# Two halves of a softmax exchange set four units of work apart, eight more buffer units, and gate tiles in another order

## The chip, the cores and the metric

The kernel runs on one core of a Trainium2 chip. A core has TensorE (PE, the matmuls; PEld is its weight load), VectorE (DVE), ScalarE (ACT), GpSimd (POOL) and SyncE (SP). Each engine works through a queue of its own in a fixed order, waits on semaphores at the head of that queue, and ACT and SP also issue DMAs from theirs. The metric is the device time of one execution in microseconds (us). The table below has the median of three timed runs and one more execution that was profiled.

## The reference

Two transformer blocks run one after the other on one sequence of 512 rows of 1024 numbers, all in float32. The first has two layers (forget-gate attention, then retention, each beside a cross-attention to 256 memory rows). The second block, where the change lies, computes:

```python
q, k, v, glu_in, gates = split(rms_norm(x, g) @ w_in)
outs, m, l = three attention groups, dilations 1, 4, 16 (4 heads each)
w = l * exp(m - max over groups of m)       # per row and head
a = sum over groups of (w * o) / sum over groups of w
y_a = a @ w_attn_out
c = silu(layer_norm(causal_conv31(val * sigmoid(gate of glu_in))))
y_c = c @ conv_pw_w
g_a, g_c = split(sigmoid(gates + b_gate))
x = x + rms_norm((g_a * y_a + g_c * y_c) @ w_out)
...                                          # then a gated feed-forward
```

The maxima `m` and the sums `l` of the three groups meet in one weight for each row and head. Group 0 (the "band") holds its rows in sequence order, 128 rows to a partition block; groups 1 and 2 (dilated) hold them by residue of the row number. So the statistics have to change layout between the groups, and the kernel does that through DRAM.

## The kernel before, in words

All large products are done as three matmuls on high and low parts of the operands (`mm3`, L208 to L215; `add_nat`, L422 to L424). Every weight cut comes in by a DMA on SP's queue into `ring_w` (L314), ACT casts its high part into `ring_hl` (L324), DVE subtracts to get the low part (L326), and then one PE unit of 24 matmuls uses it. `ring_hl` has two slots of two cuts, so casts run at most a few units ahead of PE. An evacuation into high and low parts (`evac_hl`, L204) is one ACT cast (L205) and one DVE subtraction (L206).

Side work is recorded in chains. `push([...])` makes a chain of steps, and `run_bg` takes one step from the chains after each unit; `nop` is a step that does nothing and lets a unit pass. `drain` takes all that is left. What a step records is then placed on each engine's queue by a scheduler with a model of its own of when each instruction will be ready, so the queues don't stand exactly as the steps were recorded.

For each of four heads `j` (0 to 3), the q, k and v tiles are computed, then `push_softmax(j)` starts a chain: scores of the dilated groups (their input copied by L1442, matmul L1501, maxima L1504, exponentials L1487), band scores (maxima L1524, L1487), and then the steps this case is about:

- `swap_out`, L1540 and L1541: four DMAs on ACT's queue. L1540 writes the band's maxima and sums to DRAM (`xn<-small`, 2 KB in 512 elements of 4 bytes), L1541 those of the dilated groups (`xp<-small`); each once for the maxima (k = 0) and once for the sums (k = 1).
- `swap_in`, L1549 and L1550: four DMAs on ACT's queue that read them back in the other layout (`small<-xn`, `small<-xp`). They wait at the head of ACT's queue until the write has landed.
- `weigh`: the weights, by DVE (L1556 to L1565) with one exponential on ACT for each of two halves (L1560), then the scaling of the probabilities (POOL L1574, L1577, ACT L1580).
- `tr` and `mul`: transposes (L1596; `tr_band`, L1647 to L1650, evacuated by L205 and L206) and the products with v (L1616; `pv_band`, with `mm3`). Their order on the list puts groups 1 and 2 first, the band last.

Beside these, DVE runs the pieces of the 31-tap convolution (L1418), sigmoids of ACT (L1382 for the gated linear unit, L1771 for the gates) evacuate PE's units, and `FS` is a pool of buffer units for 128x512 float32 (`arena_f`, N_F of them).

Of the kernel before, what the change touches and what calls it, by code (L numbers as in the profile page):

```python
# [33 lines left out]
TW = 384  # L34

N_R = 50
N_F = 23
N_HL = 2


# [60 lines left out]
def tile_kernel(ctx: ExitStack, tc: tile.TileContext, a: dict, out: bass.AP, stop_at=None):  # L101
    nc = tc.nc
# [6 lines left out]
    arena_r = cpool.tile([P, N_R, 512], F32R, name="arena_r")  # L109
    arena_f = cpool.tile([P, N_F, 512], F32, name="arena_f")  # L110
    ring_w = cpool.tile([P, 2, 2048], F32, name="ring_w")
# [3 lines left out]
    RS = Slots([arena_r[:, i] for i in range(N_R)], "R")  # L115
    FS = Slots([arena_f[:, i] for i in range(N_F)], "F")
    WS = Slots([ring_w[:, i] for i in range(2)], "W")
# [3 lines left out]
    def hl():  # L121
        return HL(RS.get(), RS.get())
# [50 lines left out]
    def vc(i):  # L173
        return vec[:, i : i + 1]
# [29 lines left out]
    def evac_hl(src, h, l):  # L204
        nc.scalar.copy(h, src)  # L205
        nc.vector.tensor_sub(l, src, h.bitcast(F32))  # L206

    def mm3(ps, pairs, start=True, stop=True, check=True):  # L208

        n = len(pairs)  # L210
        for k, (wh, wl, xh, xl) in enumerate(pairs):
            o = {} if check else {"skip_group_check": True}
            nc.tensor.matmul(ps, wh, xh, start=start and k == 0, stop=False, **o)  # L213
            nc.tensor.matmul(ps, wh, xl, start=False, stop=False, **o)  # L214
            nc.tensor.matmul(ps, wl, xh, start=False, stop=stop and k == n - 1, **o)  # L215
# [79 lines left out]
    def push(steps):  # L295
        c = Chain(steps)
        chains.append(c)
        return c
# [89 lines left out]
    def wsrc(w, r0, nr, c0, ncol):  # L388
        return w[r0 : r0 + nr, c0 : c0 + ncol].rearrange("(k p) c -> p k c", p=P)

    def add_proj(w, c0, x, evacs, n=512):


        def unit(i):
            def f(h, l):
                ps = PA.get()
                sl = slice(i * P, (i + 1) * P)
                mm3(ps[:, 0:n], [(h[:, k, sl], l[:, k, sl], x()[k].h[:, 0:n], x()[k].l[:, 0:n]) for k in range(KC)])
                evacs[i](ps)
                ps.free()  # L400

            return f

        ncol = P * len(evacs)
        all_jobs.append(
            Job([((A, A, slice(0, ncol)), wsrc(w, 0, D, c0, ncol))], (8, 256), CUT2[: len(evacs)],
                [unit(i) for i in range(len(evacs))])
        )
# [46 lines left out]
    def add_call(f):  # L455
        all_jobs.append(Job(None, None, None, [f]))
# [203 lines left out]
    getx = lambda: G["h"]  # L660
# [576 lines left out]
    w2 = a["w_in_2"][0]  # L1237
# [231 lines left out]
    def by_residue(ap):  # L1469

        return ap.rearrange("p (t r) -> p r t", r=4)

    def stats(j, g):

        key = ("st", j, min(g, 1))
        if key not in G:
            G[key] = SM.get()
        return G[key]
# [55 lines left out]
    def push_softmax(j):  # L1534
        def swap_out():

            n, r = stats(j, 0), stats(j, 1)
            for k in range(2):
                c = 12 * k
                nc.scalar.dma_start(xn[j, k].rearrange("(i p) -> p i", p=P), n[:, c : c + 4])  # L1540
                nc.scalar.dma_start(  # L1541
                    xp[j, k].rearrange("g (p r) -> p g r", r=4), r[:, c + 4 : c + 12].rearrange("p (g r) -> p g r", g=2)
                )

        def swap_in():
            n, r = stats(j, 0), stats(j, 1)
            for k in range(2):
                c = 12 * k
                nc.scalar.dma_start(r[:, c : c + 4], xn[j, k].rearrange("(p r) -> p r", r=4))  # L1549
                nc.scalar.dma_start(n[:, c + 4 : c + 12], xp[j, k].rearrange("g (i p) -> p (g i)", p=P))  # L1550

        def coef(g):

            st = stats(j, g)
            top, tot = st[:, 24:28], st[:, 28:32]
            nc.vector.tensor_max(top, st[:, 0:4], st[:, 4:8])  # L1556
            nc.vector.tensor_max(top, top, st[:, 8:12])
            m3 = st[:, 0:12].rearrange("p (g i) -> p g i", g=3)
            nc.vector.tensor_sub(m3, m3, top.unsqueeze(1).to_broadcast([P, 3, 4]))
            nc.scalar.activation(st[:, 0:12], st[:, 0:12], AF.Exp, scale=SCALE)  # L1560
            nc.vector.tensor_mul(st[:, 12:24], st[:, 12:24], st[:, 0:12])
            nc.vector.tensor_add(tot, st[:, 12:16], st[:, 16:20])
            nc.vector.tensor_add(tot, tot, st[:, 20:24])
            nc.vector.reciprocal(tot, tot)
            nc.vector.tensor_mul(m3, m3, tot.unsqueeze(1).to_broadcast([P, 3, 4]))  # L1565

        def norm(g):

            st = stats(j, g)
            us = G[("p", g, j)][0]  # L1570
            if g:
                u, c = us[0].ap, st[:, 4 * g : 4 * g + 4]
                u3 = u.rearrange("p (r q) -> p r q", r=4)
                nc.gpsimd.tensor_mul(u3, u3, c.unsqueeze(2).to_broadcast([P, 4, P]))  # L1574
            else:
                u3 = us[0].ap.rearrange("p (i q) -> p i q", i=2)
                nc.gpsimd.tensor_mul(u3, u3, st[:, 2:4].unsqueeze(2).to_broadcast([P, 2, 256]))  # L1577
                for i in (1, 0):
                    p = G[("p", g, j)][1][i]
                    nc.scalar.activation(p, p, AF.Copy, scale=st[:, i : i + 1])  # L1580

        def weigh():
            coef(1)
            norm(1)
            norm(2)
            coef(0)
            norm(0)
            for i in range(2):
                G.pop(("st", j, i)).free()

        def tr(g):
            u, p = G.pop(("p", g, j))
            if g:
                ps = PA.get()
                for r in range(4):
                    nc.tensor.transpose(ps[:, r * P : (r + 1) * P], p[r], ident)  # L1596
                t = FS.get()
                nc.scalar.copy(t.ap, ps.ap)
                ps.free()
                G[("pt", g, j)] = t  # L1600
            else:
                G[("pt", g, j)] = tr_band(p)
            for x in u:
                x.free()

        def mul(g):
            v = G[("v", g, j // 2)]
            pt = G.pop(("pt", g, j))
            if g == 1:
                G[("av", j)] = PA.get()  # L1610
            ps = G[("av", j)]
            if g:
                o = by_residue(ps.ap)
                for r in range(4):
                    c = (r % 2) * 256 + (j % 2) * P
                    nc.tensor.matmul(  # L1616
                        o[:, r], v[r // 2][:, c : c + P], pt[:, r * P : (r + 1) * P],
                        start=g == 1 and r == 0, stop=False, skip_group_check=True,
                    )
                pt.free()  # L1620
            else:
                pv_band(v, j % 2, pt, ps)
            if j % 2:
                for x in G.pop(("v", g, j // 2)):
                    x.free()
            if g == 0:
                ps = G.pop(("av", j))
                t = hl()
                evac_hl(ps.ap, t.h, t.l)
                ps.free()  # L1630
                G[("a", j)] = t

        push([
            swap_out, nop, swap_in, nop, weigh, nop,
            lambda: (tr(1), tr(2)), lambda: (mul(1), mul(2)), lambda: tr(0), lambda: mul(0),
        ])

# [117 lines left out]
    def add_block2():  # L1755
# [12 lines left out]
        def eg(c, f):  # L1768
            def ev(ps):
                t = FS.get()  # L1770
                nc.scalar.activation(t.ap, ps.ap, AF.Sigmoid, bias=vc(V_BG + c * 8 + f))  # L1771
                G[("sg", c, f)] = t

            return ev
# [37 lines left out]

        for t in range(4):
            add_proj(w2, 6656 + t * 256, getx, [eg(0, 2 * t), eg(0, 2 * t + 1)])
            if t == 3:
                add_call(flush)
        half_a(0)
        half_a(1)

# [20 lines left out]
            return ev  # L1840

        getc = lambda: G["c"]
        gate = lambda t: add_proj(w2, 7680 + t * 256, getx, [eg(1, 2 * t), eg(1, 2 * t + 1)])
        gate(0)
        gate(1)
        add_call(drain)
        for t in range(4):
            add_proj(a["conv_pw_w_2"][0], t * 256, getc, [ev_c(2 * t), ev_c(2 * t + 1)])
            if t < 2:
                gate(t + 2)  # L1850
            if t == 1:
                add_call(free_h)

        def free_c():
# [433 lines left out]
```

## Time and profile before

| | us |
|---|---|
| timed runs | 1913.97, 1913.65, 1907.75 (median 1913.65) |
| profiled execution | 1909.46, its span 1907.8 |
| PE busy | 1855.4 (97% of the span) |
| DVE, ACT, POOL busy | 1142.7, 825.7, 354.7 |

PE is busy nearly all the time. What is not work of PE is some 52 us in small pieces, and in the middle of the second block the four head chains are the place where PE waits. A row of a timeline gives the start, the length, the engine, the line and the operation, and in brackets how long the engine had been idle and what ended that.

### The profile page before, as it was taken

How to read it: one execution, taken by the hardware profiler on the slowest of the kernel's cores; microseconds unless marked ns; L12 is line 12 of the kernel's file. 1: busy time of each engine (PE TensorE's matmuls, PEld its weight loads, DVE VectorE, ACT ScalarE, POOL GpSimd, SP SyncE). 2: the span in 40 equal slices, each digit the busy share in tenths (PEclk: the TensorE clock that was granted, in tenths of full speed). 3: DMA queues.
4: the chain of work that ended last, by engine and by line, in shares of the span. 5: the costliest groups of instructions: out<-in, count | busy, mean ns of one | idle time of the engine just before them, and what ended most of it. 6: DMA issues, size and time to landing. Idle time of an engine off the chain costs nothing. (4 is left out here: it accounts for less than half of the span.)

```text
span 1907.8 us, 24620 instructions
## 1 busy us (share of the span) xinstructions
PE 1855.4 (97%) x9759; PEld 1588.2 (83%) x9759; DVE 1142.7 (60%) x1752; ACT 825.7 (43%) x1395; POOL 354.7 (19%) x324
## 2 busy tenths in 40 slices
PE   7899999999989999999999999989999999999998
PEld 7688888888888888898878988968888887888886
DVE  7644544344474566756569797969365386554555
ACT  5444433444354645445253324324363455333342
POOL 1110100110031133433361101010031242100101
PEclk9999999999999999999999999989999999999999
DMA  6342232232223232323223534542553213323221
GB/s 207 106 128 89 78 100 89 78 99 90 89 94 122 72 100 81 97 79 98 77 82 115 171 96 77 116 101 89 172 171 111 89 67 103 108 89 111 88 89 66
DMA packets 200373, 194.57 MB, mean 102 GB/s; under 512 B 22199, under 2 KB 171574, under 8 KB 200258
## 3 DMA queue, kind: packets, MB, share of 16 engines
q1 hardware_dynamic: 184386, 192.90, 32.4%
q10 hardware_dynamic: 15872, 0.10, 0.7%
q8 instruction: 76, 1.25, 0.3%
q14 instruction: 39, 0.32, 0.1%
HBM read 182.40 MB, written 12.94 MB: 102 GB/s over the span
## 5 line engine op out<-in xcount | busy, mean ns | idle before, releaser
L213 PE MATMUL psum<-arena_r,ring_hl 128*128 128x512 f32 (+1 forms) x1936 | 746.8, 387 | 9.5 <-ACT ring_hl L324 8.6
L215 PE MATMUL psum<-arena_r,ring_hl 128*128 128x512 f32 (+1 forms) x1936 | 741.3, 383 | 6.3 <-DVE ring_hl L326 6.3
L214 PE MATMUL psum<-arena_r,ring_hl 128*128 128x512 f32 (+1 forms) x1936 | 740.8, 383 | 3.4 <-DVE arena_r L627 2.6
L326 DVE TENSOR_TENSOR ring_hl<-ring_w,ring_hl 128x1024 fp32r<-128x1024 f32 (+2 forms) x306 | 393.9, 1294 | 284.5 <-ACT ring_hl L324 279.2
L324 ACT CAST ring_hl<-ring_w 128x1024 fp32r<-128x1024 f32 (+2 forms) x307 | 316.4, 1037 | 511.7 <-PE psum L214 330.8
L213 PEld LDWEIGHTS psum<-arena_r,ring_hl 128*128 128x128 f32 x1936 | 367.0, 190 | 79.4 <-ACT ring_hl L324 9.0
L215 PEld LDWEIGHTS psum<-arena_r,ring_hl 128*128 128x128 f32 x1936 | 366.7, 189 | 79.1 <-DVE ring_hl L326 8.5
L214 PEld LDWEIGHTS psum<-arena_r,ring_hl 128*128 128x128 f32 x1936 | 367.1, 190 | 73.1 <-DVE arena_r L627 3.3
L422 PE MATMUL psum<-ring_hl,arena_r 128*128 128x256 f32 x640 | 183.8, 287 | 2.2 <-ACT ring_hl L324 2.2
L424 PE MATMUL psum<-ring_hl,arena_r 128*128 128x256 f32 x640 | 182.9, 286 | 0.3 <-DVE ring_hl L326 0.3
L1418 DVE SCALAR_TENSOR_TENSOR arena_f<-cpad,vec,arena_f 128x512 f32<-128x512 f32 x240 | 180.5, 769 | 3.7
L423 PE MATMUL psum<-ring_hl,arena_r 128*128 128x256 f32 x640 | 182.7, 285 | 0.0
L422 PEld LDWEIGHTS psum<-ring_hl,arena_r 128*128 128x128 f32 x640 | 124.6, 195 | 3.4 <-ACT ring_hl L324 2.6
L423 PEld LDWEIGHTS psum<-ring_hl,arena_r 128*128 128x128 f32 x640 | 124.5, 195 | 0.5
L424 PEld LDWEIGHTS psum<-ring_hl,arena_r 128*128 128x128 f32 x640 | 124.3, 194 | 0.6 <-DVE ring_hl L326 0.6
L206 DVE TENSOR_TENSOR arena_r<-psum,arena_r 128x512 fp32r<-128x512 f32 (+2 forms) x136 | 78.7, 607 | 69.0 <-ACT arena_r L205 68.9
L205 ACT CAST arena_r<-psum 128x512 fp32r<-128x512 f32 (+2 forms) x136 | 66.5, 526 | 95.6 <-PE psum L215 38.3
L205 ACT CAST arena_r<-arena_f 128x512 fp32r<-128x512 f32 (+1 forms) x78 | 46.2, 598 | 116.9 <-POOL arena_f L1962 67.3
L926 POOL TENSOR_SCALAR arena_f<-arena_f,small 128x512 f32<-128x512 f32 (+3 forms) x48 | 33.9, 725 | 307.8 <-DVE small L924 302.5
L206 DVE TENSOR_TENSOR arena_r<-arena_f,arena_r 128x512 fp32r<-128x512 f32 (+1 forms) x78 | 53.3, 689 | 60.2 <-ACT arena_r L205 59.5
L606 POOL TENSOR_TENSOR arena_f<-arena_f 128x512 f32<-128x512 f32 x40 | 63.7, 1604 | 99.3 <-ACT arena_f L601 97.0
L1962 POOL TENSOR_TENSOR arena_f<-arena_f 128x512 f32<-128x512 f32 x22 | 32.0, 1455 | 262.2 <-DVE arena_f L1938 247.8
(240 smaller groups left out, 2078.0 us busy)
## 6 DMA issues: line engine op xcount, KB each, us to landing
ring_w<-in_fox_w_in SPq DMA_DIRECT2D x28, 1024.0 KB
ring_w<-in_w_in SPq DMA_DIRECT2D x22, 1024.0 KB
ring_w<-in_w_up SPq DMA_DIRECT2D x22, 1024.0 KB
ring_w<-in_w_out SPq DMA_DIRECT2D x20, 1024.0 KB
ring_w<-in_ret_w_in SPq DMA_DIRECT2D x16, 1024.0 KB
ring_w<-in_w_in SPq DMA_DIRECT2D x24, 512.0 KB
ring_w<-in_w_down SPq DMA_DIRECT2D x10, 1024.0 KB
ring_w<-in_w_mem_kv SPq DMA_DIRECT2D x8, 1024.0 KB
```

The source lines that it names most:

```text
L205: nc.scalar.copy(h, src)
L206: nc.vector.tensor_sub(l, src, h.bitcast(F32))
L213: nc.tensor.matmul(ps, wh, xh, start=start and k == 0, stop=False, **o)
L214: nc.tensor.matmul(ps, wh, xl, start=False, stop=False, **o)
L215: nc.tensor.matmul(ps, wl, xh, start=False, stop=stop and k == n - 1, **o)
L324: nc.scalar.copy(j.hv[sl], v[sl])
L326: (nc.gpsimd if j.done in j.spare else nc.vector).tensor_sub(lo, v[sl], j.hv[sl].bitcast(F32))
L422: nc.tensor.matmul(o, c.h[:, sl], h[:, k, :], start=k == 0, stop=False)
L423: nc.tensor.matmul(o, c.l[:, sl], h[:, k, :], start=False, stop=False)
L424: nc.tensor.matmul(o, c.h[:, sl], l[:, k, :], start=False, stop=k == n - 1)
L606: nc.gpsimd.tensor_add(acc, acc, t.ap)
L1418: nc.vector.scalar_tensor_tensor(t, src, wk, t, ALU.mult, ALU.add)
```

## The change

N_F goes from 23 to 31, with the memory for eight more units from a smaller scratch area of dynamic DMAs. The chain of a head gets two more empty steps between writing the statistics out and reading them in, and two more between reading them in and weighing. In the gate tiles the first goes before `flush`, and the other three are spread as the diff shows. No instruction of PE, DVE, POOL or SP is added or removed; ACT gets four more table loads, and instructions stand in another order.

```diff
--- before.py
+++ after.py
@@ -34,7 +34,7 @@
 TW = 384
 
 N_R = 50
-N_F = 23
+N_F = 31
 N_HL = 2
 
 
@@ -1631,7 +1631,7 @@
                 G[("a", j)] = t
 
         push([
-            swap_out, nop, swap_in, nop, weigh, nop,
+            swap_out, nop, nop, nop, swap_in, nop, nop, nop, weigh, nop,
             lambda: (tr(1), tr(2)), lambda: (mul(1), mul(2)), lambda: tr(0), lambda: mul(0),
         ])
 
@@ -1812,8 +1812,9 @@
 
         for t in range(4):
             add_proj(w2, 6656 + t * 256, getx, [eg(0, 2 * t), eg(0, 2 * t + 1)])
-            if t == 3:
-                add_call(flush)
+        gate = lambda t: add_proj(w2, 7680 + t * 256, getx, [eg(1, 2 * t), eg(1, 2 * t + 1)])
+        gate(0)
+        add_call(flush)
         half_a(0)
         half_a(1)
 
@@ -1840,15 +1841,13 @@
             return ev
 
         getc = lambda: G["c"]
-        gate = lambda t: add_proj(w2, 7680 + t * 256, getx, [eg(1, 2 * t), eg(1, 2 * t + 1)])
-        gate(0)
         gate(1)
+        gate(2)
         add_call(drain)
         for t in range(4):
             add_proj(a["conv_pw_w_2"][0], t * 256, getc, [ev_c(2 * t), ev_c(2 * t + 1)])
-            if t < 2:
-                gate(t + 2)
-            if t == 1:
+            if t == 0:
+                gate(3)
                 add_call(free_h)
 
         def free_c():
@@ -2273,7 +2272,7 @@
     import concourse.bacc as bacc
     from concourse.bass_utils import run_bass_kernel_spmd
 
-    nc = bacc.Bacc("TRN2", target_bir_lowering=False, num_devices=1)
+    nc = bacc.Bacc("TRN2", target_bir_lowering=False, num_devices=1, dynamic_dma_scratch_size=1024)
     arrays, aps = {}, {}
     values = {n: np.ascontiguousarray(inputs[n]) for n in _INS}
     values.update(_constants())
```

Three places on ACT's queue show it. At the exchange of head 1 (j = 1) the queue read like this from the first write of the band's statistics on, before:

```order
L1540 DMA xn<-small 128x4x1
L1487 ACT_TABLE_LOAD
L1487 ACTIVATE arena_f,small<-arena_f,small 128x256 x3
L1487 ACTIVATE arena_f,small<-arena_f,small 128x128
L1541 DMA xp<-small 128x2x4
L1540 DMA xn<-small 128x4x1
L324 CAST ring_hl<-ring_w 128x8x128
L1549 DMA small<-xn 128x4
L1550 DMA small<-xp 128x8x1
L1549 DMA small<-xn 128x4
L1550 DMA small<-xp 128x8x1
L324 CAST ring_hl<-ring_w 128x8x128 x2
```

and now, from the sigmoid that stands between the two writes (the first write stands five rows above it, ahead of the exponentials):

```order
L1382 ACTIVATE arena_f<-psum 128x512
L1540 DMA xn<-small 128x4x1
L324 CAST ring_hl<-ring_w 128x8x128
L1549 DMA small<-xn 128x4
L1560 ACT_TABLE_LOAD
L1560 ACTIVATE small<-small 128x12
L1549 DMA small<-xn 128x4
L324 CAST ring_hl<-ring_w 128x8x128
L205 CAST arena_r<-psum 128x512
L205 CAST arena_r<-psum 128x256
L1560 ACTIVATE small<-small 128x12
L205 CAST arena_r<-psum 128x128
```

The exchange of the dilated groups (L1541, L1550) has gone to an earlier place. The second write now stands behind a sigmoid, and the three evacuations L205 of `tr_band` stand behind the second read. They belong to the band of head 0: its `tr(0)` and `mul(0)` have come late enough to fall within the exchange of head 1. On PE the products of `pv_band` of head 0 stand 87 matmuls behind the last band score of head 1 now, two units of 24, 15 transposes and matmuls of `tr_band` and `mul` and a third unit of 24; before they stood ahead of it.

At the exchange of head 2 the queue read, before:

```order
L1540 DMA xn<-small 128x4x1
L1487 ACTIVATE arena_f,small<-arena_f,small 128x256 x3
L1487 ACTIVATE arena_f,small<-arena_f,small 128x128
L1549 DMA small<-xn 128x4
L1540 DMA xn<-small 128x4x1
L205 CAST arena_r<-psum 128x512
L1560 ACTIVATE small<-small 128x12
L1549 DMA small<-xn 128x4
L1560 ACTIVATE small<-small 128x12
L1580 ACTIVATE arena_f<-arena_f,small 128x256
L1580 ACTIVATE arena_f<-arena_f,small 128x128
L324 CAST ring_hl<-ring_w 128x8x128
```

and now:

```order
L1540 DMA xn<-small 128x4x1
L1487 ACTIVATE arena_f,small<-arena_f,small 128x256 x3
L1487 ACTIVATE arena_f,small<-arena_f,small 128x128
L1549 DMA small<-xn 128x4
L1540 DMA xn<-small 128x4x1
L324 CAST ring_hl<-ring_w 128x8x128
L1382 ACT_TABLE_LOAD
L1382 ACTIVATE arena_f<-psum 128x512
L1549 DMA small<-xn 128x4
L1560 ACT_TABLE_LOAD
L1560 ACTIVATE small<-small 128x12 x2
L324 CAST ring_hl<-ring_w 128x8x128
```

Between the two writes stood no cast of a weight and between the second write and the second read none either. The read of the first is still ahead of the second write, but a cast and a sigmoid have moved in ahead of the second read, and the dilated exchange and L1580 have moved away.

At the exchange of head 3 the queue read like this from the first read on, before:

```order
L1549 DMA small<-xn 128x4
L1550 DMA small<-xp 128x8x1
L1549 DMA small<-xn 128x4
L1550 DMA small<-xp 128x8x1
L324 CAST ring_hl<-ring_w 128x8x128
L1771 ACTIVATE arena_f<-psum,vec 128x512
L324 CAST ring_hl<-ring_w 128x8x128
L1560 ACT_TABLE_LOAD
L1560 ACTIVATE small<-small 128x12 x2
L1580 ACTIVATE arena_f<-arena_f,small 128x256
L1580 ACTIVATE arena_f<-arena_f,small 128x128
```

and now, from the row behind the first read on:

```order
L1560 ACT_TABLE_LOAD
L1560 ACTIVATE small<-small 128x12
L1549 DMA small<-xn 128x4
L1560 ACTIVATE small<-small 128x12
L324 CAST ring_hl<-ring_w 128x8x128
L1771 ACT_TABLE_LOAD
L1771 ACTIVATE arena_f<-psum,vec 128x512
L205 CAST arena_r<-psum 128x512
L205 CAST arena_r<-psum 128x256
L1580 ACTIVATE arena_f<-arena_f,small 128x256
L1580 ACTIVATE arena_f<-arena_f,small 128x128
L205 CAST arena_r<-psum 128x128
```

Here too the evacuations L205 of `tr_band`, those of head 2, have come to stand behind the second read (L1549); the last of them stands also behind L1580, and so behind the weights of head 3.

On the other engines the rows move along. On SP the loads into `arena_f` (such as those of L191, L981, L473, L1707) come earlier, since there are more units free. PE's order differs in some 50 rows of the prologue (transposes of vectors come earlier) and then only from the scores of head 1 to the gate tiles.

## Rows read from the trace of the kernel before

**Rows 1.** The page's first part: busy us (share of the span), instructions.

```profile
PE 1855.4 (97%) x9759; PEld 1588.2 (83%) x9759; DVE 1142.7 (60%) x1752; ACT 825.7 (43%) x1395; POOL 354.7 (19%) x324
```

**Rows 2.** Stretch: length, busy us of PE, PEld, DVE, ACT, POOL; clock; DMA.

```profile
1250.00:1300.00 50.00, 41.20 (x184) 33.53 (x183) 40.08 (x59) 16.85 (x23) 5.57 (x4) 0.90 0.30 86
```

**Rows 3.** PE's waits, 1000 to 1560 us: waiting line, releaser, total, times, longest.

```profile
PE psum L213 <- ACT ring_hl L324: 8.6, 1, 8.6
...
PE psum L1501 <- ACT arena_f L1442: 2.3, 1, 2.3
PE psum L215 <- DVE ring_hl L326: 2.2, 3, 1.2
PE psum L214 <- DVE arena_r L206: 1.0, 1, 1.0
```

**Rows 4.** Timeline of ACT and its DMA queue, head 2's exchange: start, length.

```profile
1232.35 1.05 ACT L324 CAST ring_hl<-ring_w 128x1024 fp32r<-128x1024 f32 x1
...
1233.04 0.54 ACTq L1540 DMA_DIRECT2D xn<-small  x1
...
1243.07 0.34 ACTq L1549 DMA_DIRECT2D small<-xn  x1
1243.45 0.45 ACTq L1540 DMA_DIRECT2D xn<-small  x1
...
1256.37 0.34 ACTq L1549 DMA_DIRECT2D small<-xn  x1
...
1258.21 1.03 ACT L324 CAST ring_hl<-ring_w 128x1024 fp32r<-128x1024 f32 x1
```

**Rows 5.** Timeline of PE around its longest wait there.

```profile
1250.10 0.39 PE L214 MATMUL psum<-arena_r,ring_hl 128*128 128x512 f32 x1
1250.33 0.39 PE L215 MATMUL psum<-arena_r,ring_hl 128*128 128x512 f32 x1
1259.29 0.80 PE L213 MATMUL psum<-arena_r,ring_hl 128*128 128x512 f32 x1 [8.57 <-ACT ring_hl L324]
```

**Rows 6.** Stretches right behind two of PE's waits, columns as in Rows 2.

```profile
1259.30:1264.30 5.00, 4.77 (x11) 3.34 (x12) 4.97 (x6) 4.97 (x6) 3.90 (x2) 0.51 0.39 112
...
1034.70:1039.00 4.30, 4.30 (x16) 3.61 (x17) 4.30 (x7) 1.28 (x2) 0.00 (x0) 0.60 0.00 0
```

**Rows 7.** Chain that ended last, 1150 to 1360 us: start, length, what.

```profile
1156.54 11.95 DMA xn<-small
...
1233.04 9.96 DMA xn<-small
...
1326.87 10.53 DMA xn<-small
1337.47 8.71 DMA small<-xn
```

**Rows 8.** Timeline of ACT, head 3's exchange.

```profile
1330.96 0.37 ACTq L1540 DMA_DIRECT2D xn<-small  x1
...
1343.33 1.05 ACT L324 CAST ring_hl<-ring_w 128x1024 fp32r<-128x1024 f32 x1 [9.46 <-issue]
...
1346.25 1.28 ACT L1560 ACT_TABLE_LOAD   x1 [0.35 <-DMA small<-xn]
```

**Rows 9.** Timeline of DVE, head 3's exchange.

```profile
1346.20 0.16 DVE L1556 TENSOR_TENSOR small<-small 128x4 f32<-128x4 f32 x1 [12.18 <-DMA small<-xn]
```

**Rows 10.** The page's groups: busy us, mean ns; idle before.

```profile
L326 DVE TENSOR_TENSOR ring_hl<-ring_w,ring_hl 128x1024 fp32r<-128x1024 f32 (+2 forms) x306 | 393.9, 1294 | 284.5 <-ACT ring_hl L324 279.2
L324 ACT CAST ring_hl<-ring_w 128x1024 fp32r<-128x1024 f32 (+2 forms) x307 | 316.4, 1037 | 511.7 <-PE psum L214 330.8
...
L1418 DVE SCALAR_TENSOR_TENSOR arena_f<-cpad,vec,arena_f 128x512 f32<-128x512 f32 x240 | 180.5, 769 | 3.7
...
L206 DVE TENSOR_TENSOR arena_r<-psum,arena_r 128x512 fp32r<-128x512 f32 (+2 forms) x136 | 78.7, 607 | 69.0 <-ACT arena_r L205 68.9
L205 ACT CAST arena_r<-psum 128x512 fp32r<-128x512 f32 (+2 forms) x136 | 66.5, 526 | 95.6 <-PE psum L215 38.3
```

## The prediction

> **What bounds the kernel now.** I read the page first: PE is busy 97% of the span, no other engine over 60% [rows 1]. So an edit that adds and removes no matmul can only move the some 52 us in which PE stands still, and what the clock loses behind such pauses. Next I read PE's busy time in stretches of 50 us over the second block: one falls out, with 41.2 busy of 50 at a granted clock of 0.90 [rows 2]. PE's waits from 1000 to 1560 us say why: once 8.6 us for a weight cast (L324), 2.3 for the copy L1442, 2.2 in three pieces for the low parts L326 (longest 1.2), 1.0 for L206 [rows 3]. The timeline of ACT shows where the 8.6 come from. The cast at 1232.35 is the last before the one at 1258.21, and in between ACT stands at L1549, which waits for a write to land: first from the write at 1233.04 to 1243.07, then, since the second write is issued only behind that read, from 1243.45 to 1256.37 [rows 4]. PE uses up its casts until 1250.33 and starts again at 1259.29 [rows 5]. So the wait that sets the end here is not the cast but the landing of `xn<-small`, 10 to 13 us each: 9.96, 10.53 and 11.95 in the chain of waits [rows 7], 12.9 at the second write of head 2 [rows 4]. I take 10.8.
>
> The clock adds to that. In the 5.0 us after PE's long pause it is granted at 0.51, the lower level (1.2 GHz), and after the 2.3 us pause the mean over 4.3 us is 0.60 [rows 6]. At half speed 5.0 us do the work of 2.5, so that pause costs 8.6 + 2.5 = 11.1 us; the short one loses some 1.7 (0.40 of 4.3).
>
> **What goes.** The 11.1 us at head 2; the 1.2 us for L326 at head 3, where DVE stood 12.18 us at L1556 for the read to land [rows 3, 9]; and the 1.0 us for L206, which was the band product of head 1 [rows 3]: 13.3 us. The 2.3 us at L1501 belong to head 0, whose scores stand as before; they stay.
>
> **What comes.** Below, 0 is the end of the last band score of the head whose exchange it is, and a PE unit of 24 matmuls takes 24 x 0.227 = 5.5 us (0.23 from one matmul to the next in [rows 5]). Durations: cast 1.04, L326 1.29, L205 0.53, L206 0.61, a piece of the convolution 0.77 [rows 10], a table load 1.28 [rows 8].
>
> Head 1. PE reaches `pv_band` of head 0 after 3 units and 15 short matmuls, at 17.6. The first write goes out at about 1.7. At head 3 the second write stood 4.1 us behind the first, with a table load and the exponentials between them [rows 7, 8]; here another table load and a sigmoid, which waits for the next unit's end at 5.5, come in between: 1.7 + 4.1 + 1.3 = about 7, and it lands at 7 + 10.8 = 17.8. Only then come its read, a cast (to 19) and the three L205. On DVE the low part of that cast stands ahead of the three L206, and DVE waits for the same landing, with some 3.5 us of small operations, two pieces of the convolution among them, in front: 17.8 + 3.5 + 1.3 + about 1.6 for three L206 and a piece of the convolution = 24.2. PE, with `pv_band` itself 1.4 us long, is through at 24.5 instead of 19: 5.5 us late. The bounds are the landing at 9.96 and at 12.9: 4.5 and 7.5; if DVE takes its turn earlier, 3.5.
>
> Head 3. The same with the gates' sigmoid, and a wait more. The second write goes out at about 8.5, behind a cast, a table load and a sigmoid, and lands at 19.3; the weights that stand ahead of the L206 wait also for the landing of its read, 3 to 5 us on (8.71 at the worst, in [rows 7]). DVE comes to the three L206 at about 25, the last L205 stands behind L1580, and PE is through at 26.8 instead of 19: 7.8 us late, between 5 and 11.
>
> Head 2. Here the queue gets better: two casts before the first write and one between it and the second read. PE has work until 5 x 5.5 = 27. The first write lands at 12.2, the second is issued behind its read at 12.7 and lands at 23.5; then a table load, two exponentials and the cast, to 26.4, and the low part on DVE behind the weights, 28.3 to 31. I take 2 us late; bounds 0 and 6 (landing of 12.9 twice).
>
> Tight copies. Six groups of dilated scores now stand 7 matmuls (1.6 us) behind the unit whose end L1442 waits for, and a cast and the copy take about 1.6 and a semaphore each. I take 1 us in all; bounds 0 and 4.
>
> Clock. Three pauses of 2 to 8 us; two of them should bring a stretch at the lower level, 1.7 to 2.5 us each by [rows 6]. I take 4; bounds 1 and 7.
>
> Eight more units of `arena_f`. They let loads start earlier. No wait of PE in [rows 3] is for such a load, so I put them at 0, with 2 either way: it could shorten the prologue or push more transfers against the exchange. The four table loads on ACT (4 x 1.28 [rows 8]) are in the times above where they stand in front of a write or a cast; elsewhere ACT, busy 43% [rows 1], hides them, and they would cost some of their 5 us only if a cast behind one were the next that PE needs.
>
> **Sum.** 5.5 + 7.8 + 2 + 1 + 4 = 20.3 come, 13.3 go: 7 us slower. On the profiled execution that is 1909.46 + 7 = 1916.5. This execution lies 4.2 us under the median of the timed runs; the mean of all four is 1911.2, so I forecast 1911.2 + 7 = 1918 us. The lower bounds of all terms give 3.5 + 5 + 0 + 0 + 1 = 9.5, which is 3.8 us faster; the upper ones 7.5 + 11 + 6 + 4 + 7 = 35.5, 22 slower.
>
> The write itself is the disputed price. The Trainium skill (DMA: Bandwidth & Descriptors, on the two cost components) puts a DMA at about 2.0 us fixed plus bytes over 436 GB/s, which makes 2 us of these 2 KB; by that, head 1's second write would land at 9 and nobody would wait, which is the first rival below. The trace disagrees by a factor of five, and the same page's entry on strided runs, one descriptor per element, fits better: the write is 512 elements.
>
> **Rivals.**
> 1. The wait of head 2 goes and none takes its place: faster. For it speaks that casts now stand between the waits there and that the reads of the dilated statistics are out of the way. Then all 13.3 us go: 1911.2 - 13.3 = 1898; with half of the new waits (7.5 of 15 us) and no loss of clock it would be 1905. It needs the second write to land by about 13 at heads 1 and 3, thus within 5 to 6 us of its issue; no write in [rows 4, 7] does that. Chance 0.22.
> 2. Waits of the same size take its place: 10 to 15 us in all, clock included, as when landings are near 10 and the pauses, split over three places and over single matmuls of `pv_band`, leave the clock up. 1908 to 1916. Chance 0.33.
> 3. The forecast, slower, with 0.35; and beyond it, with 0.10, a worse form: the loads that now start earlier run beside the exchanges, so that the writes take 13 and the reads 8.7 [rows 4, 7]. Heads 1, 2 and 3 then cost 2 to 3 us more each and every pause drops the clock: 1927. The Trainium skill says of this (same page, on issuing engines) that DMAs of SP and ACT run on the same 16 engines and interleave; the trace has 86 GB/s on average in the stretch of the longest landing [rows 2], which doesn't decide it.
>
> That the change doesn't do what it says belongs to the second: the empty steps count units of the recording, yet the second write is held up by a sigmoid on its own queue, so that four units of distance turn into less than three.
>
> **Range and chances.** 1904 to 1927 holds the forecast, the second rival and the near half of the first. The likeliest case alone spans 1915 to 1925. About 0.3% (5.7 us) is what a measurement here can tell from no change, seen from the median: faster 0.22, same 0.33, slower 0.45.
>
> **What would show it.** Right: PE waits for L205 or L206 at the first matmuls of `pv_band` in the exchanges of heads 1 and 3, 4 to 11 us each; the wait for L324 at head 2 is under 6; L1549 still ends ACT's longest idle times; stretches of lower clock behind the new pauses. Wrong: landings under 7 us; PE without a pause at `pv_band`; a wait of 8 us still at head 2; or a difference of more than 2 us outside of 1000 to 1400 us, which would be the buffer units.

## The result and the profile after

The changed kernel takes 1924.97 us (median of nine runs, 1919.73 to 1930.84), the kernel before 1913.65 (median of nine, 1907.75 to 1914.87). The ratio is 1.006 with a 95% interval of 1.0048 to 1.0072: slower, by some 11 us, which is clear of the noise. The profiled execution of the changed kernel took 1921.04 us, its span is 1919.3, again 11.5 more than before.

The first part of the page (busy us, share of the span, instructions) answers to [rows 1]:

```profile
PE 1860.1 (97%) x9759; PEld 1590.8 (83%) x9759; DVE 1141.6 (59%) x1752; ACT 830.4 (43%) x1399; POOL 351.8 (18%) x324
```

PE works 5 us more for the same matmuls, which is the clock, and stands still 7 us more. The stretches of 50 us answer to [rows 2], with the same columns:

```profile
1250.00:1300.00 50.00, 41.71 (x182) 34.08 (x181) 35.32 (x65) 18.66 (x30) 5.22 (x3) 0.92 0.31 81
1300.00:1350.00 50.00, 42.44 (x196) 35.41 (x196) 37.38 (x77) 23.21 (x43) 6.49 (x5) 0.88 0.51 128
```

Two stretches fall out now, with 41.7 and 42.4 busy, where before it was one with 41.2. PE's waits from 1000 to 1570 us answer to [rows 3] (waiting line, releaser, total, times, longest):

```profile
PE psum L1501 <- ACT arena_f L1442: 10.9, 3, 8.2
PE psum L213 <- ACT arena_r L205: 6.9, 1, 6.9
PE psum L215 <- DVE ring_hl L326: 3.2, 2, 2.4
PE psum L214 <- DVE arena_r L206: 3.1, 2, 2.4
```

The 8.6 us at L213 for the cast L324 are gone. In their place stand 8.2 at L1501, 6.9 at the first matmul of `pv_band` for L205, 2.4 for L206, and 2.4 for L326. What this costs in clock is seen behind the pauses (stretch: length, busy us of PE, PEld, DVE, ACT, POOL; clock; DMA):

```profile
1076.00:1081.00 5.00, 5.00 (x15) 3.97 (x16) 4.93 (x7) 0.00 (x0) 0.00 (x0) 0.66 0.77 231
...
1295.70:1300.70 5.00, 4.98 (x16) 4.30 (x17) 5.00 (x8) 0.00 (x0) 0.00 (x0) 0.50 0.00 0
1342.70:1349.00 6.30, 5.62 (x18) 4.78 (x19) 3.74 (x7) 3.30 (x7) 2.04 (x2) 0.50 0.17 51
```

The clock was 0.66 over 5.0, 0.50 over 5.0 and 0.50 over 6.3 us (5.6 of them busy): 1.7 + 2.5 + 2.8 = 7.0 us. It stays low a little longer behind the last two stretches, to 1301.9 and 1349.7, which adds 0.9: 7.9 us. Before, two such stretches cost 2.5 and 1.7 [rows 6]. The second of these, behind the 2.3 us pause of head 0, is gone: behind the same pause the clock is now 1.00 (1030.4 to 1034.8). The sum of the middle part is then: pauses 2.45 + 2.42 + 0.48 + 8.15 + 6.88 + 0.68 = 21.1 come, 8.57 + 0.23 + 0.95 + 1.21 = 11.0 go, 7.9 - 4.2 = 3.7 of clock come on top: 13.8 us. Two pauses that both kernels have frame this part. The one that now begins at 1028 us comes 4.2 us earlier than before, the one that now begins at 1529 comes 11.0 us later: 15.2 us. So 1.4 us of the middle part are not accounted for. What makes the difference of the spans smaller (11.5) lies mostly in the first 85 us, where the changed kernel's profile is 6.5 us ahead (4.2 are left at 1028); it is treated at the end.

**Head 3**, where it was forecast. Timeline of ACT and its DMA queue, then of PE (start, length, engine, line, operation, in brackets idle and what ended it):

```profile
1322.50 0.37 ACTq L1540 DMA_DIRECT2D xn<-small  x1
...
1324.72 0.69 ACT L1771 ACTIVATE arena_f<-psum,vec 128x512 f32<-128x512 f32 x1
1330.49 0.34 ACTq L1549 DMA_DIRECT2D small<-xn  x1
...
1332.73 0.34 ACTq L1549 DMA_DIRECT2D small<-xn  x1
...
1342.06 0.85 ACT L205 CAST arena_r<-psum 128x512 fp32r<-128x512 f32 x2
```

```profile
1335.43 0.39 PE L215 MATMUL psum<-arena_r,ring_hl 128*128 128x512 f32 x1
1342.69 0.58 PE L213 MATMUL psum<-arena_r 128*128 128x256 f32 x1 [6.88 <-ACT arena_r L205]
```

The second write goes out at 1322.50, and its read at 1332.73, when it has landed. The first read, of 1330.49, lands only at 1337.7 (DVE waits 4.85 us for it), the weights follow, and L205 starts at 1342.06. PE, which ran out at 1335.8, waits 6.88 and then 0.68 us.

**Head 1.** ACT and its DMA queue:

```profile
1147.89 1.28 ACT L1382 ACT_TABLE_LOAD   x1
1147.90 0.37 ACTq L1540 DMA_DIRECT2D xn<-small  x1
1149.18 0.60 ACT L1382 ACTIVATE arena_f<-psum 128x512 f32<-128x512 f32 x1
...
1157.12 0.34 ACTq L1549 DMA_DIRECT2D small<-xn  x1
```

The second write goes out at 1147.90, when the exponentials that make its sums have just ended. The table load and the sigmoid (L1382) that stand ahead of it on the queue run later, the sigmoid from 1149.18. It lands at 1157.04, 9.1 us on, and PE waits 2.42 us at `pv_band`, for L206.

**The 8.2 us at L1501**, which were not forecast at this size. DVE, then ACT, then PE:

```profile
1252.44 0.17 DVE L1559 TENSOR_TENSOR small<-small 128x12 f32<-128x12 f32 x1 [6.89 <-DMA xn<-small]
...
1264.97 0.17 DVE L1561 TENSOR_TENSOR small<-small 128x12 f32<-128x12 f32 x1 [7.14 <-ACT small L1560]
...
1271.80 4.68 DVE L1418 SCALAR_TENSOR_TENSOR arena_f<-cpad,vec,arena_f 128x512 f32<-128x512 f32 x5
...
1279.25 3.40 DVE L1418 SCALAR_TENSOR_TENSOR arena_f<-cpad,vec,arena_f 128x512 f32<-128x512 f32 x5
...
1283.70 4.06 DVE L1418 SCALAR_TENSOR_TENSOR arena_f<-cpad,vec,arena_f 128x512 f32<-128x512 f32 x6
...
1290.98 0.17 DVE L1484 TENSOR_SCALAR small<-small 128x4 f32<-128x4 f32 x1
```

```profile
1274.86 0.58 ACT L1442 COPY arena_f<-psum 128x512 f32<-128x512 f32 x1
...
1291.18 0.40 ACT L1487 ACTIVATE arena_f<-arena_f,small 128x128 f32<-128x128 f32 x1 [14.44 <-DVE small L1484]
...
1295.09 0.58 ACT L1442 COPY arena_f<-psum 128x512 f32<-128x512 f32 x1
```

```profile
1287.18 0.39 PE L213 MATMUL psum<-arena_r,ring_hl 128*128 128x512 f32 x1
1295.72 1.65 PE L1501 MATMUL psum<-arena_f 128*128 128x128 f32 x6 [8.15 <-ACT arena_f L1442]
```

At head 2's exchange DVE stands 6.9 us for the first write (until 1252.44) and then 7.14 us for L1560 on ACT, which waits for the second (until 1264.97). The casts come through and PE goes on, but the pieces of the convolution L1418 that DVE would have done meanwhile pile up. From 1267 to 1290 DVE is busy without a break, and behind that run stands L1484 of the next head's dilated scores, at 1290.98. ACT waits 14.44 us for it with L1487, and behind L1487 stands L1442, the copy that PE needs. The landing is paid by PE 33 us after it happened, two engines further on.

### The profile page after: what moved, and what is told of

Its sections match the earlier page's. It is cut to its first block, busy times and chain, and to the rows that moved or that the text cites. A ratio compares the mean times of both kernels' runs of the same rounds, so it can differ in the third digit from the quotient of the medians.

```text
span 1919.3 us, 24549 instructions
## 1 busy us (share of the span) xinstructions
PE 1860.1 (97%) x9759; PEld 1590.8 (83%) x9759; DVE 1141.6 (59%) x1752; ACT 830.4 (43%) x1399; POOL 351.8 (18%) x324
## 5 line engine op out<-in xcount | busy, mean ns | idle before, releaser
L213 PE MATMUL psum<-arena_r,ring_hl 128*128 128x512 f32 (+1 forms) x1936 | 746.3, 386 | 1.3 <-ACT arena_r L1915 0.8
L326 DVE TENSOR_TENSOR ring_hl<-ring_w,ring_hl 128x1024 fp32r<-128x1024 f32 (+2 forms) x306 | 393.8, 1293 | 302.9 <-ACT ring_hl L324 296.2
L324 ACT CAST ring_hl<-ring_w 128x1024 fp32r<-128x1024 f32 (+2 forms) x307 | 316.2, 1037 | 485.7 <-PE psum L214 304.4
L213 PEld LDWEIGHTS psum<-arena_r,ring_hl 128*128 128x128 f32 x1936 | 367.0, 190 | 71.1 <-issue 1.9
L1418 DVE SCALAR_TENSOR_TENSOR arena_f<-cpad,vec,arena_f 128x512 f32<-128x512 f32 x240 | 176.2, 769 | 1.2
L206 DVE TENSOR_TENSOR arena_r<-psum,arena_r 128x512 fp32r<-128x512 f32 (+1 forms) x136 | 79.1, 607 | 72.8 <-ACT arena_r L205 72.7
L205 ACT CAST arena_r<-psum 128x512 fp32r<-128x512 f32 (+1 forms) x136 | 66.7, 526 | 79.1 <-PE psum L215 34.4
L205 ACT CAST arena_r<-arena_f 128x512 fp32r<-128x512 f32 (+1 forms) x78 | 46.2, 598 | 119.0 <-POOL arena_f L1961 67.3
L206 DVE TENSOR_TENSOR arena_r<-arena_f,arena_r 128x512 fp32r<-128x512 f32 (+1 forms) x78 | 53.2, 687 | 60.0 <-ACT arena_r L205 59.3
```

The lines of the kernel that those rows point to most:

```text
L324: nc.scalar.copy(j.hv[sl], v[sl])
L326: (nc.gpsimd if j.done in j.spare else nc.vector).tensor_sub(lo, v[sl], j.hv[sl].bitcast(F32))
L1418: nc.vector.scalar_tensor_tensor(t, src, wk, t, ALU.mult, ALU.add)
```

## The experiments

Each kernel was timed in five rounds against the kernel before on the same chip, except for two that ran once. Ratios are to the kernel before of the same rounds. They are what to compare by: the kernel before itself had medians of 1913.65 beside the changed kernel and of 1907.53 to 1910.05 in these rounds.

**Which part of the change costs.** One part of it at a time.

Only the units (N_F and the scratch, as in the first and last piece of the diff):

```diff
-N_F = 23
+N_F = 31
-    nc = bacc.Bacc("TRN2", target_bir_lowering=False, num_devices=1)
+    nc = bacc.Bacc("TRN2", target_bir_lowering=False, num_devices=1, dynamic_dma_scratch_size=1024)
```

> Only the eight more buffer units and the smaller scratch, chain and gate tiles as before. Theory A (the units give time at the start: between 46 and 80 us the profile of the changed kernel is ahead by 6.5 us, and PE's order there differs by transposes that come earlier): 6 to 7 us faster than before, about 1907, the pauses of 1000 to 1400 us as before (8.6 us at L213 for the cast L324). Rival B (the units let loads collide with the exchanges): slower than before by 2 us or more, longer landings of the writes. Rival C (the start is faster for another reason): no difference within 2 us.

Measured: 1910.53 us, ratio 1.0006 (0.9996 to 1.0017). Theory A fell here; the time is that of rival C. PE's waits from 1000 to 1560 us:

```profile
PE psum L214 <- DVE arena_r L206: 7.2, 1, 7.2
PE psum L215 <- DVE ring_hl L326: 4.4, 2, 3.6
...
PE psum L213 <- ACT ring_hl L324: 0.8, 1, 0.8
```

The units give a microsecond or two at the start, and cost in this profile 7.2 us at the band product of head 1: with more units free, eight pieces of the convolution have come to stand on DVE between the L206 ahead of the band product and its own three, where before there were none. At head 2 less is lost (0.8 + 3.6). The sum is nothing.

Only the four empty steps:

```diff
-            swap_out, nop, swap_in, nop, weigh, nop,
+            swap_out, nop, nop, nop, swap_in, nop, nop, nop, weigh, nop,
```

> Only the four more empty steps in the chain, 23 units and gate tiles as before. Theory A (the steps cost it all): about 16 us slower than before, near 1930, with pauses of PE at L1501 (8 us), at the first matmuls of the band product in the exchanges of heads 1 and 3 (2 to 8 us each), and none at L213 for L324. Rival D (the gate tiles cost it): within 3 us of before.

Measured: 1928.65 us, ratio 1.011 (1.0093 to 1.0126), some 20 us slower. PE's waits:

```profile
PE psum L1501 <- ACT arena_f L1442: 11.4, 3, 8.2
PE psum L213 <- ACT arena_r L205: 9.5, 1, 9.5
PE psum L214 <- DVE arena_r L206: 7.9, 5, 3.7
```

The same three places as in the changed kernel. So it is the steps that cost, and rival D is out. Alone they cost more than the whole change does, 1.1% against 0.6%. In the profiles the difference lies mostly at head 3, where PE waits 9.5 us for L205 and then 3.7 for L206 (6.9 and 0.7 in the changed kernel). Beside the steps, the units or the gate tiles take off some of the cost, though neither gains anything alone (e1, e3); which of them it is was not tried.

Only the gate tiles, the two pieces of the diff from L1812 to L1853, in short:

```diff
-            if t == 3:
-                add_call(flush)
...
+        gate(0)
+        add_call(flush)
...
-        gate(0)
         gate(1)
+        gate(2)
```

> Only the gate tiles in the new order, 23 units and the chain of before. Theory A: within 2 us of before (1911 to 1916), the pause of 8.6 us at head 2 as before. Rival D (the gate tiles put sigmoids and table loads into the last exchange): 5 to 15 us slower, the pauses at the end of the attention, after 1300 us.

Measured: 1910.35 us, ratio 1.0009 (0.9998 to 1.0019): nothing, and the pause of head 2 is there as before:

```profile
PE psum L213 <- ACT ring_hl L324: 7.5, 1, 7.5
```

**Is it the landing, or the order that the steps bring?** The changed kernel with another write:

```diff
-                nc.scalar.dma_start(xn[j, k].rearrange("(i p) -> p i", p=P), n[:, c : c + 4])
+                nc.scalar.dma_start(xn[j, k].rearrange("(p i) -> p i", i=4), n[:, c : c + 4])
...
-                nc.scalar.dma_start(r[:, c : c + 4], xn[j, k].rearrange("(p r) -> p r", r=4))
+                for i, src in enumerate(xn[j, k].rearrange("(p r i) -> i p r", p=32, r=4)[i] for i in range(4)): nc.scalar.dma_start(r[32 * i : 32 * i + 32, c : c + 4], src)
```

> The changed kernel, but the band's statistics are written in 128 runs of 16 bytes in place of 512 elements of 4 bytes, and the rearranging is done by the reads (four reads of 32 partitions). PE's order is the same. Theory A (the landing of the 4-byte write holds ACT's and DVE's queues): the writes land in 2 to 4 us, the pauses at the band product and at L1501 go, 18 to 24 us faster than the changed kernel, about 1903. Rival E (the bunching of the convolution on DVE, which the new order brings, holds PE at L1501 whatever the write takes): the pauses at the band product go, but 6 to 8 us at L1501 stay, about 1912. Rival F (the elements cost the same when read): no gain, the reads land in 10 us instead, about 1925.

Measured: 1894.9 us, ratio 0.9924 (0.9907 to 0.9942): some 14 us faster than before and, by the ratios (0.9924 and 1.006), some 26 faster than the changed kernel. PE's waits:

```profile
PE psum L1501 <- ACT arena_f L1442: 2.3, 1, 2.3
PE psum L213 <- ACT arena_r L205: 1.8, 2, 1.0
```

L1501 has only the 2.3 us of head 0 that all these kernels have; 1.8 in two pieces stay for L205 at head 3. Rival E is out: with the same order of PE the pause at L1501 is gone once the write lands fast, so the convolution piled up because DVE stood. Rival F is out too: where the profile shows it, the rearranging reads land in 2.0 to 3.8 us. The gain is a little more than theory A's 18 to 24 us. The traces fit: of the changed kernel's 21.1 us of new pauses and 7.9 of clock, 2.1 us of pauses (1.8 for L205, 0.3 for L206) and two stretches at a clock of 0.66 over 5.0 us (1.7 each) are left.

**What is the distance worth once the write lands fast?** The same write in three more settings:

> Eight more units and the 16-byte writes, chain and gate tiles as before. The e4 run has shown the landing to be the price; open is what the longer chain is worth once the write lands fast. Theory G (then the distance costs nothing and brings nothing): 1893 to 1898, as e4. Theory H (the longer chain still hides some of the exchange): 3 to 8 us over e4, 1898 to 1903, with PE's pauses at head 2 (L213 for L324) or at the band product of head 1 (L206, 7 us in e1).

The edit is the diffs of e1 and e4 together on the kernel before. Measured: 1894.81 us, ratio 0.9924 (0.9908 to 0.9939).

> The kernel before with the 16-byte writes and the rearranging reads alone. Theory G: the 8.6 us at head 2 with its clock loss of 2.5 and the 1.2 at head 3 go, eight reads in place of two cost some issue time: 10 to 13 us faster than before, 1896 to 1899. Theory H: the same pauses in a smaller form stay, 3 to 6 us faster than before.

The diff of e4 alone, on the kernel before. Measured: 1894.05 us, ratio 0.9927 (0.9912 to 0.9943).

> The kernel before with the longer chain (e2) and the 16-byte writes. Theory G: the 19 us that the longer chain cost in e2 go, and it ends within 4 us of e6. If part of e2's cost were the order itself (the band product and the dilated scores behind the convolution on DVE), it would end 5 us or more over e6.

The diffs of e2 and e4 together on the kernel before. Measured: 1898.33 us, ratio 0.9949 (0.9935 to 0.9963).

With a write that lands fast the distance brings nothing: e4, with the whole change, and e6, without any of it, have the same ratio (0.9924 and 0.9927). Nearly all of what the steps cost came from the landing, as theory G says: the 20 us between e2 and before have shrunk to 4.3 between e7 and e6. This rest is just over the 4 us that G allowed. It is probably real, since only one of e6's six runs is slower than e7's fastest: e7's profile has waits of 1.3 us for L205 and 1.0 for L206 that e6's has not.

**Why does the write take 10 us?** Both explanations of the prediction, 2 us for 2 KB or 512 elements, can be told from a third by an edit that moves no instruction, only the place of the elements in DRAM:

```diff
-    xn = dpool.tile([4, 2, S], F32, name="xn")
+    xn = dpool.tile([4, 2, S, 16], F32, name="xn")
...
-                nc.scalar.dma_start(xn[j, k].rearrange("(i p) -> p i", p=P), n[:, c : c + 4])
+                nc.scalar.dma_start(xn[j, k].rearrange("(i p) z -> p i z", p=P)[:, :, 0], n[:, c : c + 4])
...
-                nc.scalar.dma_start(r[:, c : c + 4], xn[j, k].rearrange("(p r) -> p r", r=4))
+                nc.scalar.dma_start(r[:, c : c + 4], xn[j, k].rearrange("(p r) z -> p r z", r=4)[:, :, 0])
```

> The changed kernel with one edit that moves no instruction: each 4-byte element of the exchanged statistics has a place of its own in DRAM, 64 bytes from the next, so that 512 single elements are still written, but no two into the same 64 bytes (the reads then are 4-byte elements too). Theory I (the write is slow because neighbours from different partitions fall into the same short piece of DRAM and are taken one behind the other): it lands in 2 to 4 us and the kernel is as fast as e4 within 4 us, 1893 to 1899. Theory J (it is slow because it is 512 elements): it lands in 9 to 13 us as before and the time stays near 1922 to 1925.

Measured: 1891.02 us, ratio 0.9909 (0.9896 to 0.9922), the fastest of all. The row of the second write of head 1 (name, queue, count, size, us from issue to landing), first in the changed kernel, then in this one:

```profile
xn<-small ACTq DMA_DIRECT2D x1, 2.0 KB, 9.1
```

```profile
xn<-small ACTq DMA_DIRECT2D x1, 2.0 KB, 1.8
```

The same 512 elements of 4 bytes land in 1.8 us in place of 9.1. Theory J is out: it is not the number of elements. In both traces the 528 packets of this write have all been moved 1.3 us after its issue; the difference is the time from there to the landing, in which no DMA packet moves in the changed kernel for the next 4.4 us. Theory I is right in that neighbours matter; how they hold each other up is not shown. That the spaced elements take up more DRAM is not the reason by itself, since e4 gains nearly as much with the 2 KB in one piece, written in runs of 16 bytes.

Not every spaced write lands in 1.8 us. The second write of head 2 in this profile was issued at 1236.63, and ACT could issue its read only at 1242.02, 5.4 us on; the DMA engines were 0.80 busy in between. Of PE's waits there stay, longest first:

```profile
PE psum L1501 <- ACT arena_f L1442: 2.3, 1, 2.3
...
PE psum L215 <- DVE ring_hl L326: 0.8, 1, 0.8
```

Two more kernels, run once each, put 4 and 8 elements into 64 bytes, otherwise as e8:

```diff
-    xn = dpool.tile([4, 2, S, 16], F32, name="xn")
+    xn = dpool.tile([4, 2, S, 4], F32, name="xn")      # e10; 2 in e11
```

> The changed kernel with the elements 16 bytes apart, no instruction moved: 4 elements share 64 bytes in place of 16. Theory I (elements of the same 64 bytes are taken one behind the other): a landing between that of e8 and that of the changed kernel, 3 to 5 us. If the spacing matters only by 16 bytes or less: as e8, about 2 us. If all is needed or nothing: 9 to 12 us.

> The changed kernel with the elements 8 bytes apart, no instruction moved: 8 elements share 64 bytes. Theory I: a landing of 5 to 7 us, about half of the changed kernel's. If the spacing matters only by 8 bytes or less: as e8, about 2 us; if 16 elements or none: 9 to 12 us.

Measured: 1894.37 and 1895.95 us. The row of the same write, with 4 bytes every 16, then every 8:

```profile
xn<-small ACTq DMA_DIRECT2D x1, 2.0 KB, 2.9
```

```profile
xn<-small ACTq DMA_DIRECT2D x1, 2.0 KB, 3.7
```

For this one write it is 1.8, 2.9, 3.7 and 9.1 us at spacings of 64, 16, 8 and 4 bytes: the closer, the later, and by far the worst where nothing is left between them. The 3.7 is less than the 5 to 7 that theory I gave for eight elements in 64 bytes. Which size of DRAM piece it is that neighbours share isn't settled by this.

The kernel before with the spacing of 64 bytes alone:

> The kernel before with nothing but the elements of the band's statistics 64 bytes apart in DRAM; no instruction moves. Theory I, with the distance worth nothing once the write lands fast: the pauses of 8.6 us at head 2 and 1.2 us at head 3 go, 12 to 16 us faster than before, within 3 us of e8. Theory K (the four more steps or the eight more units of the change gain something now): 4 us or more slower than e8, with a pause at head 2 or 3 that e8 has not.

Measured: 1894.74 us, ratio 0.9919 (0.9901 to 0.9937). PE's waits:

```profile
...
PE psum L1501 <- ACT arena_f L1442: 2.3, 1, 2.3
PE psum L215 <- DVE ring_hl L326: 0.8, 1, 0.8
```

No pause at heads 2 and 3 is left. e8 is 3.7 us faster by the medians and some 2 by the ratios, whose intervals overlap, so whether the change is worth something on top of the spacing stays open; K isn't shown.

## Why the prediction was right, and where it was not

- **What bounds the kernel.** Right: the landing of `xn<-small` set the end of the pause at head 2. e9 moves no instruction, lets it land sooner, and the pause is gone.
- **What goes, 13.3 us.** Right: none of the three pauses is there after. Their sum with the clock is 13.5 in the traces.
- **Head 3, 7.8 us.** Right: 6.88 + 0.68 = 7.6, with the steps that end it as forecast: the read's landing, the weights, L326, L206. That the size fits is partly luck. The second write went out 5.7 us behind the last band score and not 8.5, since the sigmoid did not hold it here either (1322.50 against 1324.72), and the first read took 7.2 us and not 3 to 5.
- **Head 1, 5.5 us.** Too large: 2.42. The step that failed is that the second write waits for the sigmoid ahead of it on ACT's queue. It was issued 1.3 us before the sigmoid ran, 3.7 us after the first write and not 5.3. As the first write went out 0.9 later than forecast, this makes only 0.7 us. The rest has other terms: the landing took 9.1 us and not 10.8, and PE came to `pv_band` at 18.8 and not 17.6, as the trace has 23 short matmuls on the way there (16 of L1616, 7 of `tr_band`) where 15 were counted. What the rows show of the queue: a table load and a sigmoid that had not started did not hold the DMA behind them (PE's unit for the sigmoid had ended by 1147.1, so its input was there), while a DMA that waits (L1549) held the computations behind it.
- **Head 2, 2 us.** 0.1: PE used up its five units at 1268 us, about 27 behind the last band score as forecast, and the next low part was ready at 1268.7. The landings took 10.4 and 10.1 us, not 10.8.
- **Tight copies, 1 us.** This is the term that was mis-sized: 8.15 + 0.48. I had counted only the cast that stands between the unit's end and L1442, and not the L1487 of the head's first scores ahead of it, nor that L1487 waits for DVE. The prediction named what is queued behind ACT's waits, and did not follow what is queued behind DVE's: the pieces of the convolution, and behind them the maxima of the next head. Before, PE's own pause of 8.6 us at head 2 gave DVE that time back; once the casts were covered, nothing did. This last is read from the two traces and was not tried by itself.
- **Head 0.** Not forecast: 2.45 us for L326, though nothing around it has moved. Its first write landed 11.6 us after its issue (1049.38 to 1060.95) against 9.6 before (1053.57 to 1063.18). And PE came sooner, by the 1.7 us that the clock no longer cost behind the pause of head 0. e2 has both again (a landing of 11.1 us, a clock of 1.00, then a wait of 2.25), while e1 and e3 have a clock of 0.64 there and no such wait. Which of the two makes it was not tried.
- **Clock, 4 us.** 7.9, over three stretches. The 1.7 us behind the pause of head 0, which I had left standing, went.
- **Units, 0.** Right in the sum (e1, 1.0006).
- **The sum and the range.** For the middle part I had forecast 7.0 us net; -3.1 at head 1, -2 at head 2, -0.2 at head 3, +7.6 at the copies, +2.45 at head 0, +3.9 and -1.7 of clock and -0.2 in what goes bring it to the 13.8 of the profile, twice the forecast. The range (1904 to 1927) holds the median, near its upper end. The mechanism is the one forecast, landings that hold the queues; that the total comes so near is partly luck, as terms that were too large made up for terms that were too small or missing, and the start of the profile took off some of the rest.
- **The price of the write.** I took it from rows, which was enough for the forecast. The explanation that I preferred, that 512 elements are slow, was wrong. The Trainium skill (DMA: Bandwidth & Descriptors, two cost components) gives some 2 us as the fixed part of a DMA, fitted to DMAs that GpSimd issues; e8's row, from ACT's queue, is near it with 1.8 us for 512 elements 64 bytes apart, and the changed kernel's row, 9.1, is not, for a write that differs in the spacing alone. The entry on strided runs there, one descriptor per element, agrees with the 528 packets of this write in both traces and doesn't tell them apart.

## What to carry to other kernels

Before putting more distance between a transfer and its use, ask why the transfer takes so long: here an edit to the address pattern made a write land five times sooner (9.1 to 1.8 us), and the distance was worth nothing any more. Follow a wait on every engine that takes part in it, and in each queue as far as the next instruction that another engine needs; a stall that PE has before may be what lets a second engine catch up. And an empty step helps only where what moves into the gap doesn't itself stand behind the same transfer.

## What was not expected of the hardware

Single 4-byte elements written side by side into DRAM from different partitions land in 9 to 13 us, in both kernels and at every head. 64 bytes apart they land in 1.8 us (e8, head 1), and in up to 5.4 beside other traffic (e8, head 2).

At 48 us, PE waits for one subtraction of POOL (L271), and it takes 3.93 us in some executions and 1.35 in others. Rows of POOL and of DVE, first before, then after:

```profile
47.96 3.93 POOL L271 TENSOR_TENSOR arena_r<-arena_f,arena_r 128x512 fp32r<-128x512 f32 x1 [0.42 <-DMA arena_f<-in_conv_dw_b]
```

```profile
48.08 1.22 DVE L326 TENSOR_TENSOR ring_hl<-ring_w,ring_hl 128x1024 fp32r<-128x1024 f32 x1
```

```profile
48.10 1.35 POOL L271 TENSOR_TENSOR arena_r<-arena_f,arena_r 128x512 fp32r<-128x512 f32 x1 [0.42 <-ACT arena_r L270]
```

```profile
48.22 2.32 DVE L326 TENSOR_TENSOR ring_hl<-ring_w,ring_hl 128x1024 fp32r<-128x1024 f32 x1
```

Both engines start within 0.12 us of each other. Where POOL takes 3.93, DVE's L326 takes 1.22; where POOL takes 1.35, DVE takes 2.32. It isn't the edit: e8 and e10, with the same instructions in the same order, have 1.35 and 3.93 in their profiles, and of the thirteen profiles six have the long form. PE waits 2.8 us in it. With the lower clock behind it (0.57 over 4 us), that makes some 4.5 of the 6.5 us by which the changed kernel's profile was ahead at 85 us. e1 has the long form, and its profile was ahead by less than 2. The rest is a wait at 70 us (L782), which the units shorten from 1.77 to 0.75 us, and the lower clock behind it before (0.57 over 4 us). Which of the two engines gets through first in a given execution is open.
